# A hybrid encoder layer on one core: residual and its squares by token, gate and up alternating in the FFN's first group

## The chip, the core and the metric

The kernel runs on one core of a Trainium2 chip. The metric is the device time of one execution in microseconds, the median over several executions. The engines are named as in the profile: PE (TensorE, matrix products), DVE (VectorE), ACT (ScalarE), POOL (GpSimd), and SP, which here only issues transfers. Times inside an execution are microseconds from the start of the profiled span.

## What is computed

One transformer-like layer over 16 meta tokens and 256 sequence tokens with 2048 features, in float32. Cut to what matters here:

```python
def rms_norm(x, g):
    y = x * lax.rsqrt(jnp.mean(x * x, axis=-1, keepdims=True) + EPS)
    return y * g

h = rms_norm(x, g_mix_pre)
u = h @ w_in
...
mix = jnp.concatenate([y_a, y_b, y_c, y_d], axis=-1) @ w_out
x = x + rms_norm(mix, g_mix_post)
h = rms_norm(x, g_ffn_pre)
gate = causal_dwconv(h @ ffn_w_gate, ffn_conv_w, ffn_conv_b)
y = (jax.nn.silu(gate) * (h @ ffn_w_up)) @ ffn_w_down
return x + rms_norm(y, g_ffn_post)
```

The four mixers behind `...` are not touched. `FFN_DIM` is 5632. The result is wanted for the 256 sequence tokens alone. The convolution over three tokens needs the two tokens before them, so that from w_out on the kernel carries 258 columns: 2 meta tokens and 256 others.

## The kernel before

**Layout.** Activations lie feature-major: a tile of 128 partitions (features) by 258 columns (tokens) for each of 16 feature blocks k. `mo` holds the mixers' output after w_out, `xT` the layer's input and later the new x, `hh` and `hl` the high and low part of the normalised x times its gain. Two tensors lie token-major, [128 tokens, 2 halves i, 2048 features]: `xtok`, the residual that is added at the very end, and the DRAM input `x_tok`.

**Products.** Each float32 product is made of three passes: high weight by high activation (L202), high by low (L203), low by high (L204). A weight tile is 128 x 2048 (1 MB): 4 feature blocks of input (a chunk c) by 4 output blocks f, 48 matmuls in `tile_matmuls`. SP's queue loads it (`load`, three buffers `raw`), ACT writes its high part (`whi`, L148), DVE its low part (`wlo`, L154), each in two halves, one tile ahead of PE. Where a tile is the last of its sum (c = 3), `tile_matmuls` goes block by block through all four k, otherwise by halves.

**Order.** The stages are w_in, the mixers, w_out (16 tiles), then the norm after the mixers, the FFN in 11 groups j of four tiles of gate and four of up, the 44 tiles of w_down, the last norm and the output. Side work is written as Python generators that `step` advances between tiles. A scheduler may move instructions, but from `strict` to `strict.close()` DVE and ACT keep the written order. PSUM has four banks for `acc` tiles (gate) and four for `mx` tiles (up, transposes, statistics).

**Between w_out and the FFN.** `rstd_columns` sums the squares of `mo` by matmuls with ones (L231), DVE and ACT make the reciprocal root (L239 to L252, L246), `rstd_spread` (L255) spreads it over all partitions into the PSUM tile `mrstd`. `new_x(k)` multiplies `mo` by `mrstd` on DVE (L936) and adds it to `xT` (L937, on DVE for k below 2, otherwise on POOL). `new_h(k)` makes `hh` on ACT (L940) and `hl` on DVE (L941). `turned` transposes four 128 x 128 blocks on PE (L920) into one bank, `keep` copies that to `xtok` on ACT (L924). `keep_warm` (L302) issues products of ones whose result nobody reads.

**The first group, j = 0.** After its four gate tiles `ffn_stats` starts: 16 squares of the new x on ACT (L969, L972), added up by DVE and POOL in turn into `ssum` (L973), then the columns' sums on PE (L231), the root, and the spread (L255) into free columns of the gate banks, copied to `rstd2`. `finish(j)` multiplies the group's gate and up sums by `rstd2` and makes `yT` (L1005 to L1013). Gate and up are linear in h, so the statistics are needed only in `finish`.

**The residual.** `xtok` gets, for the features 1024 to 2047, the transposed `mo` before its norm, which `residual` multiplies by the token's rstd and adds to `x_tok` (L994). For the features 0 to 1023 it gets the transposed new x (L920 and L924 again, in the tiles of group j = 1). `x_tok` holds 1024 features of each token and is loaded by SP's queue over the memory of `mo` (L986) once the last `new_x` has read it.

Of the kernel before, what the change touches and what calls it, by code (L numbers as in the profile page):

```python
# [6 lines left out]
F32 = mybir.dt.float32  # L7
F32R = mybir.dt.float32r
AF = mybir.ActivationFunctionType
ALU = mybir.AluOpType  # L10
AX = mybir.AxisListType

P = 128
# [13 lines left out]
PRE = 4  # L27
OUT_CUTS = ((0, 256), (256, 256), (512, 512), (1024, 512), (1536, 512))
AHEAD = (1, 2, 4)
WARM = (9, 2, 2)  # L30
PIECES = (4, 2, 2, 2)
LATER = 1
BIG = 1e30
NOT_ADMISSIBLE = -3.0e38
TAKEN = -3.39e38
# [39 lines left out]
def bcast(ap, dims):  # L75
    return bass.AP(tensor=ap.tensor, offset=ap.offset, ap=[ap.ap[0], *dims])
# [3 lines left out]
def hybrid_layer(ctx: ExitStack, tc, t):  # L80
# [14 lines left out]
    def acc():  # L95
        return pacc.tile([P, 512], F32, tag="acc", name="acc")

    def mix_ps():
        return pmix.tile([P, 512], F32, tag="mx", name="mx")
# [17 lines left out]
        queue += [t["w_out"][4 * f + m] for m in range(4)]  # L117
    NJ = FT // 4
    for j in range(NJ):
        queue += [t["w_gate"][4 * j + c] for c in range(4)]  # L120
        queue += [t["w_up"][4 * j + c] for c in range(4)]
    queue += [t["w_down"][k] for k in range(FT)]
    halves = {}
    raws = {}
# [100 lines left out]
    def rstd_columns(small, sq, scale, segs, ps, meanwhile=None):  # L225

        n_seg, ng = len(segs), len(sq)
        order = [(g, j, i) for g in range(ng) for j in range(len(sq[g])) for i in (1, 2, 0)]
        for g, j, i in order:
            c0, n = segs[i]  # L230
            mm(ps[0:n, g * n_seg + i:g * n_seg + i + 1], sq[g][j][:, c0:c0 + n], ones[:, 0:1],  # L231
               start=(g, j, i) == order[0], stop=(j == len(sq[g]) - 1), skip_group_check=True)
        w = ng * n_seg
        v = small.tile([P, 4, 8], F32, tag="rs", bufs=2, name="rs")
        G.memset(v, 1.0)
        n0 = segs[0][1]
        pv = ps[:, 0:w].rearrange("p (g s) -> p g s", g=ng)
        vv = v[:, 0, 0:w].rearrange("p (g s) -> p g s", g=ng)
        V.tensor_scalar(vv[0:n0, :, 0:1], pv[0:n0, :, 0:1], scale, EPS, op0=ALU.mult, op1=ALU.add)  # L239
        V.tensor_scalar(vv[:, :, 1:n_seg], pv[:, :, 1:n_seg], scale, EPS, op0=ALU.mult, op1=ALU.add)  # L240
        rsqrt(v[:, 0, 0:w], v[:, 1, 0:w], v[:, 2, 0:w], v[:, 3, 0:w], meanwhile)
        return v[:, 2, 0:w]
# [11 lines left out]
    def rstd_spread(y, i, n, out):  # L254
        nc.tensor.transpose(out, y[0:n, i:i + 1].to_broadcast([n, P]), ident[0:n, 0:n])  # L255
# [42 lines left out]
    def keep_warm(n):  # L298

        ps = mix_ps()  # L300
        for _ in range(n):
            mm(ps[:, 0:P], ones, ones, start=True, stop=True)  # L302

    keep_warm(WARM[0])
    for c in range(3):
        load(c)
    nc.sync.dma_start(xr[3], t["xT"][:, 12:16, :])
# [609 lines left out]
    def turned(src, i, k0, ps):  # L917

        for j in range(4):
            nc.tensor.transpose(ps[:, j * P:(j + 1) * P], src[:, k0 + j, SEGQ[i + 1][0]:SEGQ[i + 1][0] + P], ident)  # L920
        return xtok[:, i, k0 * P:(k0 + 4) * P], ps

    def keep(dst, ps):
        act(dst, ps, AF.Copy)  # L924


    keep_warm(WARM[1])
    for i in range(2):
        keep(*turned(mo, i, 8, mix_ps()))
    for i, (c0, n) in enumerate(SEGQ):  # L930
        rstd_spread(y, i, n, mrstd[:, c0:c0 + n])
    later = [turned(mo, i, 12, mix_ps()) for i in range(2)]
    keep_warm(WARM[2])

    def new_x(k):
        V.tensor_tensor(mo[:, k, :], mo[:, k, :], mrstd[:, :LQ], ALU.mult)  # L936
# [27 lines left out]
    gens.append(["new_h", new_hs(), None])  # L964

    def ffn_stats(gate):
        for k in range(KT):
            if k == 0:
                pin(act(ssum, xT[:, k, :], AF.Square))  # L969
            else:  # L970
                sq = T.tile([P, LQ], F32, tag="tsq", bufs=2, name="tsq")
                pin(act(sq, xT[:, k, :], AF.Square))  # L972
                pin((G if k % 2 else V).tensor_tensor(ssum, ssum, sq, ALU.add))  # L973
            if k % 4 == 3:
                yield

        y = rstd_columns(T, [[ssum]], 1.0 / D, SEGQ, gate[3][:, 264:272])
        yield
        for i, (c0, n) in enumerate(SEGQ):
            rstd_spread(y, i, n, gate[i][:, 264:264 + n])  # L980
            act(rstd2[:, c0:c0 + n], gate[i][:, 264:264 + n], AF.Copy)

    def residual():

        x2 = bcast(mo, [[D // 2, 2], [1, D // 2]])
        nc.sync.dma_start(x2, t["x_tok"])  # L986
        for i in range(2):
            keep(*turned(xT, i, 0, acc()))
            yield
            keep(*turned(xT, i, 4, acc()))  # L990
            yield
        for i in range(2):
            dst = xtok[:, i, D // 2:D]
            V.scalar_tensor_tensor(dst, dst, y[:, i + 1:i + 2], x2[:, i, :], op0=ALU.mult, op1=ALU.add)  # L994
            yield

    feats = lambda k: (hh[:, k, :], hl[:, k, :])
    feats2 = lambda k: (hh[:, k, 2:LQ], hl[:, k, 2:LQ])
# [25 lines left out]
    tmp = F  # L1024
    for j in range(NJ):
        gate = [acc() for _ in range(4)]
        for c in range(4):
            tile_matmuls(gate, feats, list(range(4 * c, 4 * c + 4)), LQ, True, c == 0, c == 3)
        if j == 0:
            drain("new_h")  # L1030
            strict.close()
            gens.append(["ffn_stats", ffn_stats(gate), None])
        up = [mix_ps() for _ in range(4)]
        for c in range(4):
            tile_matmuls(up, feats2, list(range(4 * c, 4 * c + 4)), SEQ, True, c == 0, c == 3)
        if j == 0:
            drain("ffn_stats")
            gens.append(["residual", residual(), None])
        finish(j, gate, up)
        if j == NJ - 3:  # L1040
            drain("residual")
            tst.close()
            Y = ctx.enter_context(tc.tile_pool(name="down_in", bufs=1, side="right"))
            gpost_row = Y.tile([P, D], F32, name="gpost_row")
            G.dma_start(gpost_row, bass.AP(tensor=t["rows"].tensor, offset=t["rows"].offset + 32, ap=[[0, P], [1, D]]))
            ys = {0: ysplit(0), 1: ysplit(1)}
# [60 lines left out]
def layout(inputs):  # L1107
    import numpy as np

    f = {k: np.asarray(v) for k, v in inputs.items()}  # L1110
    a = {}
    h = np.concatenate([f["meta_tokens"], f["x"][0]], axis=0)
    a["xT"] = h.T.reshape(KT, P, L).transpose(1, 0, 2)

    a["x_tok"] = f["x"][0].reshape(2, P, D).transpose(1, 0, 2)[:, :, D // 2:]

    def cols_of(v, n):
        return v.reshape(n, P).T

    cw = f["ssd_conv_w"][0]  # L1120
    fw = f["ffn_conv_w"][0]
    i = np.arange(P)[:, None]
    mask15 = np.where(i % 2 == 0, -BIG, 0.0)
    a["cols"] = np.concatenate([
        cols_of(f["norm_mix_pre"][0], 16), cols_of(f["norm_mix_post"][0], 16), cols_of(f["norm_ffn_pre"][0], 16),
        cw.reshape(4, 8, P).transpose(2, 1, 0).reshape(P, 32), cols_of(f["ssd_conv_b"][0], 8),
        cols_of(f["ssd_norm"][0], 4), cols_of(f["pool_scale"][0], 4), f["dsa_kv_norm"][0][:, None],
        cols_of(np.repeat(f["ssd_d"][0], HD), 4),
        fw.reshape(3, FT, P).transpose(2, 1, 0).reshape(P, 3 * FT), cols_of(f["ffn_conv_b"][0], FT), mask15,
        i % 2 == np.array([0, 1]), i % 16 <= np.array([14, 15]), i // 16 == np.arange(H)], axis=1).astype(np.float32)  # L1130
    a["rows"] = np.concatenate([f["ssd_dt_bias"][0], f["fox_f_bias"][0], f["ssd_a_log"][0], np.zeros(8, np.float32),
                                f["norm_ffn_post"][0]])[None]
    p = i.T
    head = np.where(p % 32 < 4, 8 + p // 32 * 2 + p % 32 // 2, -1)
    a["consts"] = np.concatenate([np.eye(P), i <= p, i == head, i == p // 16, i == p % 16], axis=1).astype(np.float32)

    def tiles(w):
        k, n = w.shape
        return w.reshape(k // 512, 4, P, n // 512, 512).transpose(3, 0, 2, 1, 4).reshape(-1, P, 2048)

    w_in = f["w_in"][0]
    parts = []
    for g in ORDER:
        for c, n in W_IN_GROUPS[g]:
            parts.append(np.zeros((D, n), np.float32) if c is None else w_in[:, c:c + n])
    a["w_in"] = tiles(np.concatenate(parts, axis=1))
    w_out = f["w_out"][0]
    a["w_out"] = tiles(np.concatenate([w_out[P * MIX_ROWS[m]:P * MIX_ROWS[m] + 512] for m in MIX_ORDER], axis=0))
    a["w_gate"] = tiles(f["ffn_w_gate"][0])
    a["w_up"] = tiles(f["ffn_w_up"][0])  # L1150
    a["w_down"] = f["ffn_w_down"][0].reshape(FT, P, D)
    a["w_uk"] = f["dsa_w_uk"][0].transpose(1, 0, 2).reshape(P, 512)
    a["w_uv"] = f["dsa_w_uv"][0].transpose(1, 0, 2).reshape(P, 512)
    a["pool_w"] = f["pool_w"][0].transpose(1, 0, 2)
    return {k: np.ascontiguousarray(v) for k, v in a.items()}
# [15 lines left out]
```

## Time and profile before

| what | value |
|---|---|
| median of three executions | 1162.54 us (1160.34 to 1163.70) |
| the profiled execution | 1161.08 us |
| its span, first to last instruction | 1159.3 us |
| what lies around the span | 1.8 us |
| PE busy, matmuls | 1136.5 us, 98% |
| DVE busy | 721.6 us, 62% |
| ACT busy | 541.6 us, 47% |
| POOL busy | 56.0 us, 5% |
| mean granted clock of PE | 0.993 of full speed |
| moved by the DMA queues | 207.34 MB, 179 GB/s in the mean |

The busy shares are averages over very different stages. A time at which PE waits or runs at a lower granted clock is found in the timeline of PE and in the windows, which give for a stretch the busy time of each engine and the granted clock (1.00 is 2.4 GHz, 0.50 is 1.2 GHz).

### The profile page before, as it was taken

Reading aid. Unit: us, or ns where it says so; the run is one execution under the profiler, and the core shown is the slowest. Engines: PE = TensorE matmul, PEld = TensorE weight load, DVE = VectorE, ACT = ScalarE, POOL = GpSimd, SP = SyncE. Lnnn points to the kernel's source line nnn. Section 1 sums busy time; section 2 is a strip of 40 time slices with the busy share of each in tenths; the row PEclk is TensorE's granted clock in tenths of the full one; section 3 lists DMA queues with packets and bytes.
Section 4 is the critical chain, followed back from the end, with each engine's and each line's share of the span. In section 5 each row is a group of like instructions: output and inputs, shape, how many; then the busy total and the mean of one; then the engine's idle time right before and its main releaser. Section 6 shows DMA issues by size and latency. Waiting matters only on the chain.

```text
span 1159.3 us, 19938 instructions
## 1 busy us (share of the span) xinstructions
PE 1136.5 (98%) x8331; PEld 1068.6 (92%) x8331; DVE 721.6 (62%) x1150; ACT 541.6 (47%) x767; POOL 56.0 (5%) x64
## 2 busy tenths in 40 slices
PE   7999999999999989999999999999999999999997
PEld 7999989998999989999999999999999888888885
DVE  8885675778755876655565566555655655445564
ACT  6434363564544655544444444444444444444452
POOL 6000010000000430000000000000000000000000
PEclk9999999999999999999999999999999999999998
DMA  7644444435655354555555554555555555555542
GB/s 271 215 146 146 166 149 164 146 115 180 219 191 183 144 208 150 214 183 182 182 183 183 184 182 179 190 186 183 182 193 187 190 182 182 184 192 196 190 181 73
DMA packets 32762, 207.34 MB, mean 179 GB/s; under 512 B 3712, under 2 KB 4896, under 8 KB 9376
## 3 DMA queue, kind: packets, MB, share of 16 engines
q1 hardware_dynamic: 30528, 198.80, 48.0%
q0 software_dynamic: 1568, 6.48, 1.8%
q8 instruction: 65, 1.06, 0.4%
q10 hardware_dynamic: 576, 0.79, 0.2%
q14 instruction: 25, 0.20, 0.1%
HBM read 203.93 MB, written 2.12 MB: 178 GB/s over the span
## 4 chain that ended last, share of the span: by engine, by line
PE 63%; DVE 1%; POOL 0%; ACT 0%; issue 0%; DVEq 0%; ACTq 0%; POOLq 0%
PE mx L203 7%; PE mx L202 7%; PE mx L204 7%; PE acc L204 7%; PE acc L203 7%; PE acc L202 7%; PE acc L1060 4%; PE acc L1061 4%; PE acc L1059 4%; PE mx L1061 3%; PE mx L1060 3%; PE mx L1059 3%; POOL ssum L973 0%; DVE yo L1089 0%; DVE yo L1103 0%
## 5 line engine op out<-in xcount | busy, mean ns | idle before, releaser
L154 DVE TENSOR_TENSOR wlo<-raw,whi 128x1024 fp32r<-128x1024 f32 (+2 forms) x373 | 455.7, 1226 | 343.4 <-ACT whi L148 342.1
L148 ACT ACTIVATE whi<-raw 128x1024 fp32r<-128x1024 f32 (+2 forms) x373 | 386.8, 1046 | 476.2 <-PE acc L203 226.2
L203 PE MATMUL acc<-hl,whi 128*128 128x258 f32 x704 | 199.2, 283 | 1.0 <-DVE hl L941 0.9
L203 PE MATMUL mx<-hl,whi 128*128 128x256 f32 x704 | 199.3, 283 | 0.0
L202 PE MATMUL mx<-hh,whi 128*128 128x256 f32 x704 | 199.2, 283 | 0.0
L204 PE MATMUL acc<-hh,wlo 128*128 128x258 f32 x704 | 199.1, 283 | 0.0
L204 PE MATMUL mx<-hh,wlo 128*128 128x256 f32 x704 | 198.7, 282 | 0.0
L202 PE MATMUL acc<-hh,whi 128*128 128x258 f32 x704 | 198.2, 283 | 0.2 <-ACT hh L940 0.2
L202 PE MATMUL acc<-xh,whi 128*128 128x272 f32 (+1 forms) x576 | 171.6, 298 | 1.0 <-ACT whi L148 1.0
L204 PE MATMUL acc<-xh,wlo 128*128 128x272 f32 (+1 forms) x576 | 166.3, 291 | 4.3 <-DVE wlo L154 4.3
L203 PE MATMUL acc<-xl,whi 128*128 128x272 f32 (+1 forms) x576 | 166.9, 290 | 0.5 <-DVE xl L315 0.5
L203 PEld LDWEIGHTS acc<-hl,whi 128*128 128x128 f32 x704 | 133.3, 189 | 1.8 <-DVE hl L941 1.6
L203 PEld LDWEIGHTS mx<-hl,whi 128*128 128x128 f32 x704 | 133.8, 190 | 0.0
L204 PEld LDWEIGHTS mx<-hh,wlo 128*128 128x128 f32 x704 | 133.7, 190 | 0.0
L202 PEld LDWEIGHTS mx<-hh,whi 128*128 128x128 f32 x704 | 133.4, 189 | 0.0
L202 PEld LDWEIGHTS acc<-hh,whi 128*128 128x128 f32 x704 | 132.5, 189 | 0.4 <-ACT hh L940 0.4
L204 PEld LDWEIGHTS acc<-hh,wlo 128*128 128x128 f32 x704 | 132.8, 189 | 0.0
L202 PEld LDWEIGHTS acc<-xh,whi 128*128 128x128 f32 x576 | 110.5, 192 | 7.1 <-issue 4.6
L204 PEld LDWEIGHTS acc<-xh,wlo 128*128 128x128 f32 x576 | 109.7, 192 | 5.5 <-DVE wlo L154 5.0
L203 PEld LDWEIGHTS acc<-xl,whi 128*128 128x128 f32 x576 | 110.4, 192 | 1.7 <-issue 0.9
L1061 PE MATMUL acc<-wlo,yh 128*128 128x512 f32 x176 | 69.6, 396 | 0.0
L1060 PE MATMUL acc<-whi,yl 128*128 128x512 f32 x176 | 69.6, 396 | 0.0
(375 smaller groups left out, 1506.5 us busy)
## 6 DMA issues: line engine op xcount, KB each, us to landing
raw<-w_gate SPq DMA_DIRECT2D x44, 1024.0 KB, 4.8
raw<-w_up SPq DMA_DIRECT2D x44, 1024.0 KB, 4.8
raw<-w_down SPq DMA_DIRECT2D x44, 1024.0 KB, 4.8
raw<-w_in SPq DMA_DIRECT2D x32, 1024.0 KB, 4.8
raw<-w_out SPq DMA_DIRECT2D x16, 1024.0 KB, 4.8
raw<-w_in SPq DMA_DIRECT2D x6, 512.0 KB, 7.8
xT<-xT POOLq DMA_DIRECT2D x1, 2064.0 KB, 12.0
xr<-xT SPq DMA_DIRECT2D x4, 272.0 KB, 7.2
```

The costliest lines, as they stand in the source:

```text
L148: act(hi[:, c], src, AF.Copy)
L154: V.tensor_tensor(lo, src, hi, ALU.subtract)
L202: mm(accs[f][:, :n], hi[:, c], xh, start=st, stop=False)
L203: mm(accs[f][:, :n], hi[:, c], xl, start=False, stop=False)
L204: mm(accs[f][:, :n], lo[:, c], xh, start=False, stop=en)
L1059: mm(o, yh, hi[:, c], start=(k == 0), stop=False)
L1060: mm(o, yl, hi[:, c], start=False, stop=False)
L1061: mm(o, yh, lo[:, c], start=False, stop=(k == FT - 1))
```

## The change

The changed kernel does three things. (1) All 16 blocks of `mo` are transposed between w_out and the FFN (32 transposes, where there were 16), and the 16 transposes of the new x in group j = 1 are gone, and so are the two calls of `keep_warm` between w_out and the FFN. (2) `x_tok` has all 2048 features (2 MB), POOL's queue loads it, and `ffn_stats` makes the residual by token on DVE, squares it on ACT with a sum along the row, and joins to that the sums of the two meta columns, which come from `xT`. (3) The first group takes its tiles in the order gate 0, gate 1, up 0, up 1, gate 2, gate 3, up 2, up 3, and `ffn_stats` starts after the fourth of these. Behind the places named, lines move on by two or three.

```diff
+FFN_ORDER = ([(w, c) for h in (0, 2) for w in ("w_gate", "w_up") for c in (h, h + 1)],
+             [(w, c) for w in ("w_gate", "w_up") for c in range(4)])
...
-        queue += [t["w_gate"][4 * j + c] for c in range(4)]
-        queue += [t["w_up"][4 * j + c] for c in range(4)]
+        queue += [t[w][4 * j + c] for w, c in FFN_ORDER[min(j, 1)]]
...
-    keep_warm(WARM[1])
-    for i in range(2):
-        keep(*turned(mo, i, 8, mix_ps()))
+    for k0 in (0, 4):
+        for i in range(2):
+            keep(*turned(mo, i, k0, mix_ps()))
     for i, (c0, n) in enumerate(SEGQ):
         rstd_spread(y, i, n, mrstd[:, c0:c0 + n])
-    later = [turned(mo, i, 12, mix_ps()) for i in range(2)]
-    keep_warm(WARM[2])
+    keep(*turned(mo, 0, 8, mix_ps()))
+    later = [turned(mo, i, k0, mix_ps()) for i, k0 in ((1, 8), (0, 12), (1, 12))]
...
     def ffn_stats(gate):
-        for k in range(KT):
-            if k == 0:
-                pin(act(ssum, xT[:, k, :], AF.Square))
-            else:
-                sq = T.tile([P, LQ], F32, tag="tsq", bufs=2, name="tsq")
-                pin(act(sq, xT[:, k, :], AF.Square))
-                pin((G if k % 2 else V).tensor_tensor(ssum, ssum, sq, ALU.add))
-            if k % 4 == 3:
-                yield
-
-        y = rstd_columns(T, [[ssum]], 1.0 / D, SEGQ, gate[3][:, 264:272])
+        x2 = bcast(mo, [[D, 2], [1, D]])
+        G.dma_start(x2, t["x_tok"])
+        for _ in range(3):
+            yield
+        sums = HP.tile([P, 3, 2], F32, name="sums")
+        junk = HP.tile([P, D // 2], F32, name="junk")
+        for half in range(2):
+            c = slice(half * D // 2, (half + 1) * D // 2)
+            for i in range(2):
+                dst = xtok[:, i, c]
+                V.scalar_tensor_tensor(dst, dst, y[:, i + 1:i + 2], x2[:, i, c], op0=ALU.mult, op1=ALU.add)
+                act(junk, dst, AF.Square, accum_out=sums[:, half, i:i + 1])
+            yield
+
+        sq = HP.tile([P, KT, 2], F32, name="sq")
+        act(sq, xT[:, :, 0:2], AF.Square)
+        V.tensor_reduce(sums[:, 2, :], sq.rearrange("p k t -> p t k"), axis=AX.X, op=ALU.add)
+        mm(gate[3][0:2, 264:265], sums[:, 2, :], ones[:, 0:1], start=True, stop=True, skip_group_check=True)
+        v = HP.tile([P, 4, 8], F32, name="rs2")
+        G.memset(v, 1.0)
+        V.tensor_tensor(v[:, 1, 1:3], sums[:, 0, :], sums[:, 1, :], ALU.add)
+        V.tensor_scalar(v[:, 0, 1:3], v[:, 1, 1:3], 1.0 / D, EPS, op0=ALU.mult, op1=ALU.add)
+        V.tensor_scalar(v[0:2, 0, 0:1], gate[3][0:2, 264:265], 1.0 / D, EPS, op0=ALU.mult, op1=ALU.add)
+        rsqrt(v[:, 0, 0:3], v[:, 1, 0:3], v[:, 2, 0:3], v[:, 3, 0:3])
         yield
         for i, (c0, n) in enumerate(SEGQ):
-            rstd_spread(y, i, n, gate[i][:, 264:264 + n])
+            rstd_spread(v[:, 2, 0:3], i, n, gate[i][:, 264:264 + n])
             act(rstd2[:, c0:c0 + n], gate[i][:, 264:264 + n], AF.Copy)
-
-    def residual():
...
+        up = None
+        for n, (w, c) in enumerate(FFN_ORDER[min(j, 1)]):
+            if w == "w_gate":
+                tile_matmuls(gate, feats, list(range(4 * c, 4 * c + 4)), LQ, True, c == 0, c == 3)
+            else:
+                up = up or [mix_ps() for _ in range(4)]
+                tile_matmuls(up, feats2, list(range(4 * c, 4 * c + 4)), SEQ, True, c == 0, c == 3)
+            if j == 0 and n == 3:
+                drain("new_h")
+                strict.close()
+                gens.append(["ffn_stats", ffn_stats(gate), None])
...
-    a["x_tok"] = f["x"][0].reshape(2, P, D).transpose(1, 0, 2)[:, :, D // 2:]
+    a["x_tok"] = f["x"][0].reshape(2, P, D).transpose(1, 0, 2)
```

The compiled programs show where the scheduler put things. PE between w_out and the FFN, before (L920 is a transpose, L231 the sums of squares, L255 the spread, L302 a product of ones):

```order
L302 MATMUL mx<-ones 128x128 x2
L920 MATMUL mx<-cst,mo 128x128
L231 MATMUL mx<-ones,slast 128x1 x2
L231 MATMUL mx<-ones,slast 2x1
L920 MATMUL mx<-cst,mo 128x128 x7
L255 MATMUL mx<-cst,rs 128x2
L255 MATMUL mx<-cst,rs 128x128 x2
L920 MATMUL mx<-cst,mo 128x128 x8
L302 MATMUL mx<-ones 128x128 x2
```

The same place now; the lines are L922, L233, L257:

```order
L922 MATMUL mx<-cst,mo 128x128 x5
L233 MATMUL mx<-ones,slast 128x1 x2
L233 MATMUL mx<-ones,slast 2x1
L922 MATMUL mx<-cst,mo 128x128 x11
L257 MATMUL mx<-cst,rs 128x2
L257 MATMUL mx<-cst,rs 128x128 x2
L922 MATMUL mx<-cst,mo 128x128 x16
```

Sixteen transposes now stand ahead of the spread and sixteen behind it, where eight and eight stood.

PE in the third FFN tile, which is now up 0, with numbers (`mx_4564` to `mx_4567` are up's four banks, `whi_4492` and `wlo_4493` the first half of the tile):

```order
2762 L204 MATMUL mx_4566<-hh_4339,whi_4492 128x256
2763 L205 MATMUL mx_4566<-hl_4340,whi_4492 128x256
2764 L206 MATMUL mx_4566<-hh_4339,wlo_4493 128x256
2765 L204 MATMUL mx_4567<-hh_4339,whi_4492 128x256
2766 L205 MATMUL mx_4567<-hl_4340,whi_4492 128x256
2767 L206 MATMUL mx_4567<-hh_4339,wlo_4493 128x256
```

The tile begins with number 2747, and number 2765, its nineteenth matmul, is the first that writes up's fourth bank; that bank is the one in which `mrstd` lies, which DVE reads in all sixteen of `new_x`. In the kernel before, up's first matmul stood two tiles later.

DVE around the residual, before, behind the last `hl` (L994 is the residual, two instructions for half of the features; numbers run on from the program's start):

```order
486 L154 TENSOR_TENSOR wlo_4615<-raw_4546,whi_4614 128x1024
487 L154 TENSOR_TENSOR wlo_4643<-raw_4546,whi_4642 128x1024
488 L994 SCALAR_TENSOR_TENSOR xtok_4333<-xtok_4333,rs_4317,mo_3190 128x1024 x2
489 L154 TENSOR_TENSOR wlo_4678<-raw_4612,whi_4677 128x1024
490 L973 TENSOR_TENSOR ssum_3191<-ssum_3191,tsq_4709 128x258
491 L154 TENSOR_TENSOR wlo_4716<-raw_4612,whi_4715 128x1024
```

And now (L980 is the residual, four instructions for all features):

```order
486 L156 TENSOR_TENSOR wlo_4637<-raw_4568,whi_4636 128x1024
487 L156 TENSOR_TENSOR wlo_4665<-raw_4568,whi_4664 128x1024
488 L986 TENSOR_REDUCE sums_4810<-sq_4878 128x2
489 L156 TENSOR_TENSOR wlo_4696<-raw_4634,whi_4695 128x1024
490 L980 SCALAR_TENSOR_TENSOR xtok_4333<-xtok_4333,rs_4317,mo_3190 128x1024 x2
491 L156 TENSOR_TENSOR wlo_4725<-raw_4634,whi_4724 128x1024
492 L980 SCALAR_TENSOR_TENSOR xtok_4333<-xtok_4333,rs_4317,mo_3190 128x1024 x2
493 L156 TENSOR_TENSOR wlo_4755<-raw_4693,whi_4754 128x1024
```

Number 491, the low half of the sixth FFN tile's second half, stands behind the first pair that reads `x_tok`. In this part of the program POOL's order is now the last additions of `new_x`, then the issue of the load of `x_tok`; the eight additions of L973 on POOL are gone.

## Rows read from the trace of the kernel before

**Rows 1.** the page, busy time of the engines

```profile
PE 1136.5 (98%) x8331; PEld 1068.6 (92%) x8331; DVE 721.6 (62%) x1150; ACT 541.6 (47%) x767; POOL 56.0 (5%) x64
```

**Rows 2.** PE's waits: waiter, releaser, total us, times, longest us

```profile
PE mx L573 <- DVE s L570: 2.0, 1, 2.0
...
PE acc L203 <- DVE hl L941: 0.9, 1, 0.9
```

**Rows 3.** windows: stretch, us, busy us (instructions), granted clock, DMA share, GB/s

```profile
400.86:414.30 13.44, 12.41 (x98) 11.91 (x97) 13.36 (x18) 5.67 (x8) 3.39 (x4) 1.00 0.58 201
...
414.30:442.44 28.14, 25.81 (x203) 25.33 (x202) 17.16 (x32) 17.01 (x34) 9.65 (x8) 0.94 0.48 172
...
174.00:176.00 2.00, 2.00 (x10) 2.00 (x10) 0.86 (x2) 1.28 (x3) 0.30 (x1) 0.50 0.65 184
...
434.00:436.00 2.00, 2.00 (x11) 2.00 (x10) 0.00 (x0) 0.00 (x0) 0.00 (x0) 0.50 0.29 119
```

**Rows 4.** timeline of PE, w_out to FFN: start, us, instruction, count, [idle before]

```profile
383.86 0.71 PE L302 MATMUL mx<-ones 128*128 128x128 f32 x4
...
386.70 0.55 PE L255 MATMUL mx<-cst,rs 2*128 2x2 f32 x3 [0.65 <-DVE rs L252]
...
387.09 1.04 PE L920 MATMUL mx<-cst,mo 128*128 128x128 f32 x8
...
388.77 0.74 PE L202 MATMUL acc<-hh,whi 128*128 128x258 f32 x4 [0.20 <-ACT hh L940]
```

**Rows 5.** timeline of ACT, the same stretch

```profile
385.67 1.07 ACT L924 ACTIVATE xtok<-mx 128x512 f32<-128x512 f32 x2
...
388.21 0.51 ACT L940 ACTIVATE hh<-xT,cols 128x258 fp32r<-128x258 f32 x1 [1.47 <-DVE xT L937]
```

**Rows 6.** timeline of DVE, the first FFN group

```profile
404.19 0.41 DVE L936 TENSOR_TENSOR mo<-mo,mx 128x258 f32<-128x258 f32 x1
...
405.06 1.76 DVE L154 TENSOR_TENSOR wlo<-raw,whi 128x1024 fp32r<-128x1024 f32 x1
...
411.75 2.47 DVE L994 SCALAR_TENSOR_TENSOR xtok<-xtok,rs,mo 128x1024 f32<-128x1024 f32 x2
...
414.74 1.23 DVE L154 TENSOR_TENSOR wlo<-raw,whi 128x1024 fp32r<-128x1024 f32 x1 [0.53 <-ACT whi L148]
...
433.74 0.16 DVE L252 SCALAR_TENSOR_TENSOR rs<-rs 128x3 f32<-128x3 f32 x1
...
441.94 0.43 DVE L1005 TENSOR_TENSOR gs<-acc,rstd 128x258 f32<-128x258 f32 x1
```

**Rows 7.** timeline of PE, the end of the first group's statistics

```profile
431.11 0.73 PE L231 MATMUL acc<-ones,ssum 128*128 128x1 f32 x6 [2.33 <-POOL ssum L973]
...
436.33 0.58 PE L255 MATMUL acc<-cst,rs 2*128 2x2 f32 x3
```

**Rows 8.** timeline of PE, the fourth gate tile of group j = 1

```profile
459.72 0.28 PE L202 MATMUL acc<-hh,whi 128*128 128x258 f32 x1
...
462.51 0.66 PE L920 MATMUL acc<-cst,xT 128*128 128x128 f32 x4
...
467.63 0.28 PE L202 MATMUL mx<-hh,whi 128*128 128x256 f32 x1
```

**Rows 9.** timeline of POOL, its last two additions of new_x

```profile
403.94 1.80 POOL L937 TENSOR_TENSOR xT<-xT,mo 128x258 f32<-128x258 f32 x2 [1.50 <-DVE mo L936]
```

**Rows 10.** DMA issues: what, queue, count, KB each, us to landing

```profile
mo<-x_tok SPq DMA_DIRECT2D x1, 1024.0 KB, 5.3
...
gpost_row<-rows POOLq DMA_DIRECT2D x1, 1024.0 KB, 5.9
...
xT<-xT POOLq DMA_DIRECT2D x1, 2064.0 KB, 12.0
...
e<-drow POOLq DMA_DIRECT2D x1, 1024.0 KB, 7.0
```

More of the change, by code (lines that the diff above doesn't have):

```diff
@@ L29 @@
 AHEAD = (1, 2, 4)
-WARM = (9, 2, 2)
+WARM = 9
 PIECES = (4, 2, 2, 2)
 LATER = 1
+FFN_ORDER = ([(w, c) for h in (0, 2) for w in ("w_gate", "w_up") for c in (h, h + 1)],
+             [(w, c) for w in ("w_gate", "w_up") for c in range(4)])
 BIG = 1e30
@@ L302, in keep_warm @@
             mm(ps[:, 0:P], ones, ones, start=True, stop=True)
-    keep_warm(WARM[0])
+    keep_warm(WARM)
     for c in range(3):
@@ L978, in ffn_stats @@
+        V.tensor_scalar(v[0:2, 0, 0:1], gate[3][0:2, 264:265], 1.0 / D, EPS, op0=ALU.mult, op1=ALU.add)
+        rsqrt(v[:, 0, 0:3], v[:, 1, 0:3], v[:, 2, 0:3], v[:, 3, 0:3])
         yield
         for i, (c0, n) in enumerate(SEGQ):
-            rstd_spread(y, i, n, gate[i][:, 264:264 + n])
+            rstd_spread(v[:, 2, 0:3], i, n, gate[i][:, 264:264 + n])
             act(rstd2[:, c0:c0 + n], gate[i][:, 264:264 + n], AF.Copy)
-    def residual():
[L985 to L995, printed above, removed]
@@ L1026, in hybrid_layer @@
         gate = [acc() for _ in range(4)]
[L1027 to L1035, printed above, removed]
+        up = None
[9 more added lines that the diff above has]
+                gens.append(["ffn_stats", ffn_stats(gate), None])
         if j == 0:
             drain("ffn_stats")
-            gens.append(["residual", residual(), None])
         finish(j, gate, up)
         if j == NJ - 3:
-            drain("residual")
             tst.close()
```

## The prediction

> **What bounds the kernel now.** I read the page first: PE is busy for 98% of the span and DVE for 62% [rows 1]. So work moved between DVE, ACT and POOL is worth nothing by itself. Time is won where PE waits, runs at a lower clock, or does work that can go. The view of PE's waits lists few after w_out: 0.9 us for `hl` in the gate tiles, and a longer one that the timeline of PE shows as 2.33 us before L231, for `ssum` of POOL [rows 2, 7]. The windows, cut at the first matmul of FFN tiles, give the stages [rows 3]. Fifth to eighth tile (up of group 0) take 28.14 us. The pace to hold against that is the first three gate tiles of group 1: from 442.44, where the window ends, to 459.72 [rows 3, 8], 17.28 / 3 = 5.76 us a tile, 0.120 a matmul of 258 columns. A tile of up, with 256 columns, is then 5.76 x 256/258 = 5.72 us. Four are 22.9, so this stage loses 5.2: the wait, six small L231, a spread, and a fall of the clock: 432 to 436 us holds a stretch at a granted clock of 0.50 (1.2 GHz) [rows 3]. The third and fourth gate tile lose 13.44 - 2 x 5.76 = 1.9 us [rows 3]. The fourth gate tile of group 1 lasts 467.63 - 459.72 = 7.91 us, 2.1 above pace, for the 16 transposes within it [rows 8].
>
> **Transition (w_out to FFN).** Sixteen more transposes come in, four products of ones go (two times some 0.7 us; one shown) [rows 4]. A transpose costs 1.04/8 = 0.13 us [rows 4]. Ahead of the spread, eight more take about 1.0 us against 0.7 for the products that go, and 0.65 us of PE's idle time stood there [rows 4]: the spread stays at 386.7. Behind it 16 take 2.1 us where 8 and the products lasted until 388.57, the start of the 0.20 idle before 388.77 [rows 4]. By PE alone they would end at 389.2; four wait at a time for an ACT copy (1.07 the pair [rows 5]) that frees their bank. The next to gate on `hl` is DVE, which has lost nothing; the first `hh` moves by one ACT copy at most, 0.53, with 1.47 idle ahead of it [rows 5]. Bounds 0 and 0.6; I take a loss of 0.1, since the second matmul group waited for `hl` anyway.
>
> **Third and fourth tile.** With up 0 and up 1 in their place, PE needs `hl` of k = 0 to 7 only, and the waits for the later ones, 1.9 us, go. Something else takes their place: up's fourth bank is `mrstd`'s, which DVE reads last at 404.19 + 0.41 = 404.60 [rows 6]. The nineteenth matmul of the third tile wants it: 400.86 [rows 3] + 18 x 0.119 = 403.0. That is a new wait of 1.6 us. Behind it two tiles of up are 11.44 + 1.6 = 13.04 instead of 13.44: gain 0.4, less the 0.1 above; bounds 0 to 1.9. The wait lies between one of 0.92 (`hl`) behind which no lower clock shows and one of 1.97 behind which 174 to 176 ran at 0.50 [rows 2, 3]. I take no fall, and keep the fall as a rival.
>
> **Statistics.** Three small L231, a pass over ACT and fifteen additions go. In their place PE has one small matmul: 0.73/6 [rows 7], with its filling 0.2. The spread keeps its 0.4. The four tiles, two of gate and two of up, last 2 x 5.76 + 2 x 5.72 + 0.6 = 23.6 instead of 28.14 [rows 3]: **gain 4.5**. For that DVE must be done when the spread comes, by the compiled order 24 matmuls into the eighth tile. In before DVE came from L231 (431.11) to L252's end, 433.90, in 2.8 us with one `wlo` between [rows 6, 7]; now the matmul stands right before those 24, whose 2.9 us cover that. If this cover fails, PE waits some tenths.
>
> **x_tok.** The load leaves POOL after its last addition, 403.94 + 1.80 = 405.74 [rows 9]. Before, SP's queue brought 1 MB in 5.3 us; POOL's queue brought 1 MB in 5.9 and 7.0, and 2 MB of `xT` in 12.0 [rows 10]. Doubled and added: it lands between 405.74 + 10.6 = 416.3 and 405.74 + 14.0 = 419.7, by `xT` at 417.7. The DVE order puts `wlo` of the sixth tile's second half behind the first pair of residuals: 2.47 + 1.23 = 3.7 us after the landing [rows 6]. PE wants it in the ninth matmul of the sixth tile (a last tile of gate goes through all k of a block): 400.86 + 13.04 + 0.1 + 5.76 + 8 x 0.12 = 420.7. So PE waits from a landing at 417.0 on. Bounds 0 and 2.7; I take 0.3, between what the SP row and the `xT` row give. Other `wlo` behind the second pair come 1 us or more before they are needed. The four squares on ACT have as many columns as the sixteen before and lie beside PE.
>
> Here the Trainium skill speaks, in "DMA: Bandwidth & Descriptors", "Anatomy of one DMA — SWDGE (gpsimd) path": some 2 us fixed and then 436 GB/s, by which 2 MB would land in an estimated 6.8 us and the 0.3 would be 0. The row of `xT`, 12.0 us, disagrees.
>
> **Group 1.** Its 16 transposes go: 7.91 - 5.76, **gain 2.1** [rows 8]. The eight copies on ACT have moved to the transition, where they are counted.
>
> **Finish of group 0.** It shares DVE and ACT with the splits, as before. `gs` of the fourth block ended at 442.37 [rows 6], 0.07 us before tile 9 began. Now everything is some 5 us earlier, PE included, so this is as tight as before: PE wants the fourth gate bank 32 matmuls into its tile, 3.8 us later. Bounds 0 and 1.6; I take 0.
>
> **Sum.** -0.1 + 0.4 + 4.5 - 0.3 + 2.1 = 6.6 us. Against the profiled execution, 1161.08, that is 1154.5; against the median of the runs, 1162.54, it is 1155.9. I take the middle of these two, 1161.8, as the kernel's time, and so forecast **1155.2 us**. What can be told from no change is 0.3%, 3.5 us: faster is below 1158.3, slower above 1165.3.
>
> **Rivals.**
>
> *Clock falls at the new wait.* If 1.6 us of idle time on PE is enough, a stretch of matmuls behind it goes at 1.2 GHz. The stage with the 2.33 us wait prices that: 5.2 lost, less the wait itself, 0.7 of L231 and 0.4 of the spread, leaves 1.8. Then 1157.0. For it: 1.6 is nearer to 1.97 than to 0.92. Against: the wait falls into a stretch with PE otherwise full. Chance 0.22.
>
> *Finish is late.* The third and fourth `gs` come behind a `wlo` and the load of the Silu table, and PE waits up to 1.6 in group 1's first tile: 1156.8. Against: PE reaches that bank late. Chance 0.08.
>
> *x_tok comes at the slowest rate.* By the 7.0 row it lands at 419.7, PE waits 2.7 instead of 0.3 and the clock falls for 1.8: gain 6.6 - 4.2 = 2.4, time 1159.4, within 0.3%. For it: three weight tiles of 1 MB are on the way at the same time. Chance 0.14.
>
> *x_tok comes so late that the kernel is slower.* DVE is busy without a gap until 411.8, its first residual row [rows 6]. If POOL gets to send its transfer only then, the load lands at 411.8 + 12.0 = 423.8, and with half a weight tile's time in front (2.4) at 426.2. PE then waits 9.2 instead of 0.3 and the clock falls for 1.8: 6.6 - 10.7 = 4.1 lost, 1165.9. It decides from the landing: behind 422.1 (a wait of 5.1) nothing is gained, behind 425.6 the kernel is slower by over 0.3%. For it: `wlo` took 1.76 us while POOL added and 1.23 when it did not [rows 6], so the two hinder each other. Against: POOL's additions hold POOL, a transfer's issue needs it briefly; `gpost_row` landed in 5.9 beside a DVE that was splitting weights. Chance 0.06.
>
> The Trainium skill has this in "SBUF — State Buffer", "SBUF: two separate sides": transfers issued from GpSimd have their descriptors written by GpSimd, which DVE's two-port instructions lock out, whereas SP's are safe. The two lengths of `wlo` agree with such a shared port; the 5.9 of `gpost_row` shows no lock.
>
> That the change does not do what it says can't be excluded for the alternation alone: it swaps one wait for another, which is in the sum, at 0.4.
>
> **Chances.** Forecast 0.50, the four rivals 0.22, 0.08, 0.14, 0.06. Faster by over 0.3%: 0.50 + 0.22 + 0.08 = 0.80. Within: 0.14. Slower: 0.06. The range goes down by the 0.3 of x_tok, by 0.6 of the third tile's wait and by the runs' spread of about 1.5 around their median: 1152.8. Up it holds the first three rivals and a bit of spread: 1160.0.
>
> **What would show it.** Right: first gate matmul within 0.3 of 388.8; a wait of 1.6 before an `mx` matmul at about 404.6, clock 1.00 behind it; no wait for `ssum`, fifth to eighth tile 23.6 to 24; no transposes (L922) behind the first gate matmul; group 1's gate tiles 5.76 each. Wrong: a landing of `x_tok` behind 418 with a wait for `wlo` in the sixth tile; a clock of 0.50 between 404 and 412; a wait for `gs` in group 1's first tile; a first gate matmul behind 389.4.

## The result and the profile after

Over seven executions the median went from 1162.93 to 1155.11 us. The ratio is 0.9941 with a 95% interval of 0.9921 to 0.9960: faster by 4.7 to 9.2 us. One of the seven executions of the changed kernel took 1476.17 us at a granted clock of 0.694 and is left out of the ratio. The forecast was 1155.2 in a range of 1152.8 to 1160.0.

The profiled execution has a span of 1154.3 us, 5.0 below before. What lies ahead of the change differs by chance, in code that is the same: the first sum of the norm after w_out (L231, now L233) starts at 384.77 instead of 383.31. Of before, PE's timeline:

```profile
383.31 0.62 PE L231 MATMUL mx<-ones,ssum 128*128 128x1 f32 x6
```

So all that follows is measured from that first sum, on PE's timeline, to the first `up` matmul of group 1: the **stretch**. It holds everything that the change touches. In before it is 467.63 [rows 8] - 383.31 = 84.32 us, now 462.51 - 384.77 = 77.74: 6.58 us less. What lies behind it is the same, 1159.3 - 467.63 = 691.7 and 1154.3 - 462.51 = 691.8.

The windows of the changed kernel: FFN tiles 3 and 4, 5 to 8, and the gate tiles of group 1, then two windows around the new wait (columns as in [rows 3], which has the first two stages of before):

```profile
402.29:415.47 13.18, 11.73 (x98) 11.52 (x97) 12.27 (x18) 6.19 (x9) 3.95 (x5) 1.00 0.72 275
...
415.47:439.25 23.78, 23.78 (x199) 23.46 (x198) 16.52 (x25) 14.18 (x22) 0.56 (x1) 1.00 0.80 291
...
439.25:462.51 23.26, 23.26 (x194) 23.20 (x193) 18.73 (x34) 14.91 (x23) 0.00 (x0) 1.00 0.48 167
...
404.00:406.00 2.00, 0.61 (x6) 0.40 (x4) 2.00 (x5) 1.35 (x2) 0.65 (x1) 1.00 0.24 29
...
406.00:408.00 2.00, 1.94 (x16) 1.94 (x17) 2.00 (x3) 1.32 (x4) 1.70 (x3) 1.00 0.76 270
```

13.18 stands against 13.44, 23.78 against 28.14, 23.26 against the 25.19 between 442.44 [rows 3] and 467.63 [rows 8]. Around the new wait PE was busy for 0.61 of 2 us, and the granted clock stayed at 1.00.

PE's timeline of the changed kernel at the places of [rows 4] and [rows 7], with the new wait between:

```profile
384.77 0.62 PE L233 MATMUL mx<-ones,ssum 128*128 128x1 f32 x6
...
388.11 0.55 PE L257 MATMUL mx<-cst,rs 2*128 2x2 f32 x3 [0.21 <-DVE rs L254]
...
388.50 1.95 PE L922 MATMUL mx<-cst,mo 128*128 128x128 f32 x16
...
390.20 0.74 PE L204 MATMUL acc<-hh,whi 128*128 128x258 f32 x4
...
404.33 0.28 PE L206 MATMUL mx<-hh,wlo 128*128 128x256 f32 x1
...
406.06 0.39 PE L204 MATMUL mx<-hh,whi 128*128 128x256 f32 x1 [1.45 <-DVE mo L938]
...
432.82 0.19 PE L987 MATMUL acc<-ones,sums 128*2 128x1 f32 x2
...
435.97 0.58 PE L257 MATMUL acc<-cst,rs 2*128 2x2 f32 x3
...
462.51 0.28 PE L204 MATMUL mx<-hh,whi 128*128 128x256 f32 x1
```

From the first sum to the first gate matmul: 390.20 - 384.77 = 5.43 us, before 388.77 [rows 4] - 383.31 = 5.46, with 16 transposes more. The wait for `ssum` is gone, the spread at 435.97 has no wait, and a wait of 1.45 us for DVE's last reading of `mrstd` is new.

DVE, POOL and the load of `x_tok` in the changed kernel, to compare with [rows 6, 9, 10]:

```profile
405.59 0.41 DVE L938 TENSOR_TENSOR mo<-mo,mx 128x258 f32<-128x258 f32 x1
...
416.31 2.48 DVE L980 SCALAR_TENSOR_TENSOR xtok<-xtok,rs,mo 128x1024 f32<-128x1024 f32 x2 [1.30 <-DMA mo<-x_tok]
...
407.45 0.58 POOL L971 DMA_DIRECT2D mo<-x_tok  x1 [0.30 <-POOL xT L939]
...
mo<-x_tok POOLq DMA_DIRECT2D x1, 2048.0 KB, 8.8
```

The load lands 8.8 us behind its issue; DVE stands idle for it for 1.30 us, PE does not.

### The profile page after: what moved, and what is told of

Read it like the earlier page. It is cut to its first block, busy times and chain, and to the rows that moved or that the text cites. A ratio compares the mean times of both kernels' runs of the same rounds, so it can differ in the third digit from the quotient of the medians.

```text
span 1154.3 us, 19891 instructions
## 1 busy us (share of the span) xinstructions
PE 1132.6 (98%) x8319; PEld 1065.5 (92%) x8319; DVE 721.3 (62%) x1147; ACT 540.7 (47%) x760; POOL 47.4 (4%) x57
## 4 chain that ended last, share of the span: by engine, by line
PE 77%; DVE 3%; ACT 1%; issue 1%; DVEq 0%; ACTq 0%
PE acc L204 11%; PE acc L206 11%; PE acc L205 11%; PE mx L204 7%; PE mx L205 7%; PE mx L206 7%; PE acc L1062 4%; PE acc L1063 4%; PE acc L1061 4%; PE mx L1062 3%; PE mx L1063 3%; PE mx L1061 3%; DVE wlo L156 1%; DVE mo L938 0%; DVE hl L943 0%
## 5 line engine op out<-in xcount | busy, mean ns | idle before, releaser
L1061 PE MATMUL acc<-whi,yh 128*128 128x512 f32 x176 | 69.6, 396 | 0.0
```

What stands on the lines that cost most here:

```text
L1061: mm(o, yh, hi[:, c], start=(k == 0), stop=False)
```

## The experiments

All runs are compared over the stretch and three of its stages, read off PE's timeline in one profile each. The transition from the first sum to the first gate matmul (5.43 to 5.47 us) and the first two FFN tiles (12.08 to 12.09) are the same everywhere and are left out.

| kernel | tiles 3, 4 | tiles 5 to 8 | gate, group 1 | stretch | ratio of time to before (95%) |
|---|---|---|---|---|---|
| before | 13.44 | 28.14 | 25.19 | 84.32 | |
| changed | 13.18 | 23.78 | 23.26 | 77.74 | 0.9941 (0.9921 to 0.9960) |
| changed, again (e8) | 13.17 | 23.78 | 23.26 | 77.73 | 0.9946 (0.9929 to 0.9962) |
| without the alternation (e1) | 13.44 | 23.69 | 23.27 | 77.92 | 0.9935 (0.9915 to 0.9955) |
| alternation alone (e5) | 13.20 | 25.13 | 25.19 | 81.08 | 0.9973 (0.9960 to 0.9986) |
| transposes alone (e7) | 13.45 | 32.59 | 23.08 | 86.63 | 1.0018 (1.0002 to 1.0033) |
| alternation and transposes (e11) | 13.18 | 26.96 | 23.09 | 80.74 | 0.9986 (0.9969 to 1.0003) |
| fourth block last (e3; e9) | 11.91; 11.89 | 23.78; 23.78 | 23.25; 23.24 | 76.46; 76.43 | 0.9936 (0.9917 to 0.9955); 0.9947 (0.9928 to 0.9966) |
| banks turned, no effect (e4) | 13.22 | 23.78 | 23.25 | 77.76 | 0.9948 (0.9928 to 0.9969) |
| x_tok on SP (e2) | 13.21 | 23.79 | 23.27 | 77.79 | 0.9962 (0.9947 to 0.9977) |
| x_tok late (e6) | 13.19 | 29.96 | 23.27 | 83.93 | 1.0012 (0.9997 to 1.0027) |
| bank wanted earlier (e10) | 15.75 | 23.78 | 23.25 | 80.30 | 0.9971 (0.9961 to 0.9980) |

**Without the alternation (e1).** `FFN_ORDER[0]` is that of the other groups:

```diff
-FFN_ORDER = ([(w, c) for h in (0, 2) for w in ("w_gate", "w_up") for c in (h, h + 1)],
+FFN_ORDER = ([(w, c) for w in ("w_gate", "w_up") for c in range(4)],
```

> Everything of the change but the alternation: group 0 takes gate 0 to 3, then up 0 to 3. Theory (the alternation only swaps one wait for another): third and fourth FFN tile 13.4 us, with the waits for hl back and no wait for mrstd's bank, against 13.2 with the change; fifth to eighth tile 23.8, fourth gate tile of group 1 5.8; time 1155.4, within 1 us of the changed kernel. Rival (the alternation makes the room in which the statistics are hidden): fifth to eighth tile 25 us or more with a wait of PE for wlo, the spread or rstd2; time 1157 or more.

PE's timeline of this kernel has the old wait back, and no wait for the bank:

```profile
406.20 0.39 PE L205 MATMUL acc<-hl,whi 128*128 128x258 f32 x1 [0.92 <-DVE hl L943]
```

The stretch is 0.18 us longer than with the change. In the changed kernel the alternation swaps one wait for another and is worth next to nothing, as the theory said.

**The alternation alone (e5).** Before, with the new `FFN_ORDER` and the loop over it, and nothing else.

> The kernel before with the alternation alone. Theory: the 0.9 us wait for hl becomes one of 1.5 us for mrstd's bank in the third tile, third and fourth tile 13.2 us; the wait for ssum (2.3 us) and the low clock behind it stay, fifth to eighth tile 28; transposes in group 1 stay, 25.2 for its gate tiles; time 0.3 us below the kernel before, not to be told from it. Rival (the alternation carries the gain): fifth to eighth tile 24 to 25, time 1158.

The theory failed here: the stretch is 3.24 us shorter than before, not 0.3. PE's timeline shows the bank's wait as expected, but no wait for `ssum` any more, and 0.60 us for the spread in its place:

```profile
403.14 0.39 PE L204 MATMUL mx<-hh,whi 128*128 128x256 f32 x1 [1.48 <-DVE mo L938]
...
427.20 0.73 PE L233 MATMUL acc<-ones,ssum 128*128 128x1 f32 x6
...
431.56 0.58 PE L257 MATMUL acc<-cst,rs 2*128 2x2 f32 x3 [0.60 <-DVE rs L254]
```

ACT's timeline says why. In before, the split and the first square on ACT, and the last addition on POOL:

```profile
413.65 1.06 ACT L148 ACTIVATE whi<-raw 128x1024 fp32r<-128x1024 f32 x1 [5.31 <-PE acc L203]
...
414.62 0.40 ACT L969 ACTIVATE ssum<-xT 128x258 f32<-128x258 f32 x1
...
429.60 1.46 POOL L973 TENSOR_TENSOR ssum<-ssum,tsq 128x258 f32<-128x258 f32 x1 [0.90 <-ACT tsq L972]
```

and in this kernel:

```profile
409.77 1.06 ACT L150 ACTIVATE whi<-raw 128x1024 fp32r<-128x1024 f32 x1 [1.80 <-PE mx L205]
...
410.74 0.40 ACT L971 ACTIVATE ssum<-xT 128x258 f32<-128x258 f32 x1
...
426.38 0.76 POOL L975 TENSOR_TENSOR ssum<-ssum,tsq 128x258 f32<-128x258 f32 x1 [0.61 <-DVE ssum L975]
```

In before, the split ahead of the first square waits 5.31 us for PE to give a `whi` buffer back: the fourth tile, the last of gate, goes block by block through all four k, so both halves are needed to the tile's end. In the alternated order the fourth tile is an up tile that is not the last of its sum and goes by halves, and the wait is 1.80. Measured from the first sum, the first square starts at 410.74 - 381.79 = 28.95 instead of 414.62 - 383.31 = 31.31, 2.4 us earlier. From there to the end of the last addition the chain is as long as before, 427.14 - 410.74 = 16.40 us against 431.06 - 414.62 = 16.44, so `ssum` is ready 2.4 us earlier. That is the 2.33 us that PE waited for it, and without that wait the clock stays up (1.00 in every window from 424 to 440 us).

**The transposes alone (e7).** The transition of the change and the residual by token for all features (four L994, 2 MB of `x_tok` on POOL's queue), with the old squares, additions and order.

> The transposes and the residual by token for all features (2 MB of x_tok on POOL's queue), but the old squares, additions and order. Theory: transition unchanged at 5.4 us from the first sum to the first gate matmul, group 1's gate tiles 23.0 instead of 25.2, the wait for ssum stays at 2.3 to 5 us (two more residual instructions of 1.2 us each stand in DVE's order among the additions), fifth to eighth tile 28 to 31; time 1161 to 1163.5, a gain of 2.1 at most. Rival (the 16 transposes moved to the transition cost PE there what they save in group 1): transition 7.5 us, time 1163 to 1165.

The transition takes 5.43 us with the 16 transposes more, and the gate tiles of group 1 are 2.11 us shorter, as the theory had it. The wait for `ssum` grows beyond what was expected. Of this kernel, PE, and ahead of it the first square, the residual and the last addition:

```profile
434.67 1.14 PE L231 MATMUL acc<-ones,ssum 128*128 128x1 f32 x6 [6.04 <-POOL ssum L973]
...
414.46 0.40 ACT L969 ACTIVATE ssum<-xT 128x258 f32<-128x258 f32 x1
...
414.84 2.97 DVE L993 SCALAR_TENSOR_TENSOR xtok<-xtok,rs,mo 128x1024 f32<-128x1024 f32 x2 [3.18 <-DMA mo<-x_tok]
...
433.15 1.46 POOL L973 TENSOR_TENSOR ssum<-ssum,tsq 128x258 f32<-128x258 f32 x1 [0.91 <-ACT tsq L972]
```

The residual stands in DVE's order ahead of the additions, waits 3.18 us for `x_tok`, and the additions wait with it; two more residuals stand among them further on. The chain from the first square to the last addition takes 434.61 - 414.46 = 20.15 us, 3.71 more than before, and by the same 3.71 PE's wait grows, from 2.33 to 6.04. Tiles 5 to 8 take 4.45 us more than before. By itself this part makes the kernel slower.

**Alternation and transposes, old statistics (e11).** The two edits above together.

> The alternation and the transposes, with the old squares and additions: all of the change but the sums by token. If the parts simply add up from the two runs that had one part each, the first sum to the first up tile of group 1 takes 84.3 - 3.2 + 2.3 = 83.4 us. Theory (the old chain of additions is long, and x_tok's later landing stands in DVE's order among them, but the alternation starts it 2.4 us earlier): wait of PE for ssum 1 to 4 us, stretch 79 to 83. Rival (with alternation the old statistics are hidden as well, and the sums by token bring nothing): stretch 78 us or less, no wait for ssum.

PE, the first square, the first pair of residuals, the last addition, and two windows behind PE's wait:

```profile
432.50 0.72 PE L233 MATMUL acc<-ones,ssum 128*128 128x1 f32 x6 [1.89 <-POOL ssum L975]
...
414.23 0.41 ACT L971 ACTIVATE ssum<-xT 128x258 f32<-128x258 f32 x1
...
416.83 2.99 DVE L995 SCALAR_TENSOR_TENSOR xtok<-xtok,rs,mo 128x1024 f32<-128x1024 f32 x2 [0.18 <-DMA mo<-x_tok]
...
431.71 0.74 POOL L975 TENSOR_TENSOR ssum<-ssum,tsq 128x258 f32<-128x258 f32 x1 [0.61 <-DVE ssum L975]
...
432.00:434.00 2.00, 1.50 (x13) 1.45 (x14) 1.46 (x2) 2.00 (x3) 0.45 (x1) 1.00 0.66 279
...
434.00:436.00 2.00, 2.00 (x20) 2.00 (x18) 2.00 (x4) 0.61 (x2) 0.00 (x0) 1.00 0.13 29
```

The stretch, 80.74 us, is shorter than the two parts added up give (83.4). The earlier start alone does not explain that, since it is in the alternation's 3.2 already. The rows show two things more: the chain from the first square to the last addition is 432.45 - 414.23 = 18.22 us long instead of 20.15, with the residual waiting 0.18 us for `x_tok` instead of 3.18, and the wait of 1.89 us has no lower clock behind it. The sums by token bring 80.74 - 77.74 = 3.0 us on top of it, and 86.63 - 77.92 = 8.7 where the alternation is missing.

**The fourth block last (e3, e9).** In the first tile of up, the twelve matmuls of the fourth block come behind the 36 of the other three:

```diff
+            elif wait_f3:
+                for kk in range(2):
+                    for f in range(3):
+                        pair(f, part, kk)
+                if part == 1:
+                    for k in range(4):
+                        pair(3, k // 2, k % 2)
             else:
```

> The changed kernel, with the twelve matmuls of the fourth block of up 0 behind the 36 of the other three blocks in that tile. Theory (the 1.5 us wait there is for mrstd's bank alone, and nothing else is late behind it): no wait for the bank, third and fourth tile 11.5 to 11.7 us instead of 13.2, the rest as with the change; time 1153.6, ratio to before 0.992. Rival (something else is late next: hl for gate 2, wlo, or x_tok): third and fourth tile as said, but a new wait of about 1.5 us in the fifth or sixth tile, time 1155.

> The kernel with the twelve matmuls of the fourth block last in up 0, beside the changed kernel on the same chip. Theory: the stretch from the first sum to the first up tile of group 1 is 76.2 us against 77.6, and the median 1.4 us lower; the intervals of the two will overlap, since each is wide by 4 us. Rival (the 1.5 us are given back later in the span): medians the same and the part behind that stretch longer by about 1.4.

The wait for the bank is gone in both profiles, and 0.18 us for `wlo` stand in the tile (here of e3):

```profile
404.59 0.39 PE L206 MATMUL mx<-hh,wlo 128*128 128x256 f32 x1 [0.18 <-DVE wlo L156]
```

The stretch is 1.3 us shorter than that of the changed kernel, and what lies behind it is as long (691.7 to 691.8 us in e3, e8 and e9). So nothing is late behind it and nothing is given back. The medians (1153.42 beside 1153.13 for the changed kernel on the same chip) do not resolve 1.3 us. By the traces this is the shortest version.

> The changed kernel itself, beside the next one on the same chip. From the first sum of the norm after w_out to the first up tile of group 1: 77.6 us as in its first profile; time 1154 to 1156.

Its stretch repeats to 0.01 us. Its median, 1153.13, is below what was expected; the kernel before took 1159.92 on the same chip, and 1162.93 where the change was first measured.

**A longer wait for the bank (e4, e10).** The first try turned the list of up's banks:

```diff
-                up = up or [mix_ps() for _ in range(4)]
+                if not up:
+                    up = [mix_ps() for _ in range(4)]
+                    up = up[3:] + up[:3] if j == 0 else up
```

> The changed kernel with up's four banks turned by one, so that mrstd's bank is wanted by the first matmul of the third tile and not by its nineteenth. Theory (an idle time of PE of 1.5 us costs only itself here, one of 2 us and more also a stretch at 1.2 GHz): wait 3.4 to 3.7 us, granted clock near 0.5 in some 2 to 4 us behind it, third and fourth tile 13.2 + 2.1 + 1.8 = 17.1 us; time 3.9 above the changed kernel, 1159. Rival (the clock does not fall for a single wait of this length): 15.3 us, time 1157.

In the trace the wait stands at the same place in the tile all the same, 402.78 - 399.00 = 3.78 us behind its start (3.77 in the changed kernel), and is 1.48 us long: the edit did not do what was meant. So this run tells nothing on the clock, and is one more repeat of the changed kernel. The second try pinned the matmuls of that tile in the order of the blocks (`late` off for it):

> The changed kernel with the first half of up 0 in the order of its blocks, kept by a pin, so that mrstd's bank is wanted by the tenth matmul and not by the nineteenth. Theory (the wait lasts until DVE's last reading of mrstd wherever PE meets it; of this length it costs the clock too): wait 2.5 us; clock of 0.5 for about 3.5 us behind it; third and fourth tile 13.2 + 1.8 = 15.0 us (nine matmuls come behind the wait instead of ahead of it, which adds 1.1 by itself, the low clock 1.8: 16.1 at most); time 2 to 3 above the changed kernel. Rival (the clock stays): 14.3 us, time 1.1 above it.

PE's timeline and two windows of it:

```profile
407.05 0.38 PE L205 MATMUL mx<-hh,whi 128*128 128x256 f32 x1 [2.53 <-DVE mo L939]
...
408.00:410.00 2.00, 2.00 (x14) 2.00 (x13) 2.00 (x4) 1.42 (x3) 0.72 (x2) 0.65 1.17 434
...
410.00:412.00 2.00, 2.00 (x12) 2.00 (x11) 2.00 (x5) 0.28 (x1) 0.00 (x0) 0.50 0.86 320
```

The wait is 2.53 us, and the clock falls behind it. Tiles 3 and 4 take 2.57 us more: nine matmuls that now stand behind the wait, 1.08, and 1.5 for the low clock. This is the rival of the fallen clock, at a wait one microsecond longer than the one of the change.

**x_tok on SP's queue (e2).** `nc.sync.dma_start` in place of `G.dma_start`.

> The changed kernel with x_tok on SP's queue, between the weight tiles, instead of POOL's. Theory (the queue does not matter as long as the landing is in time): issue near 407 behind the last new_x, landing 5.5 to 10 us later, no wait of PE for wlo in the fifth or sixth tile, first sum to the first up tile of group 1 77.6 us as with the change; time within 1.5 us of the changed kernel. Rival A (DVE holds up what GpSimd has to write for its own transfers): landing 3 us or more earlier than with POOL's queue, 6 us after the issue. Rival B (SP stands still until mo is free and the weights behind it come late): a wait of PE for wlo or whi of 1 us or more in the seventh tile, time 1156 or more.

The load takes 8.2 us instead of 8.8:

```profile
mo<-x_tok SPq DMA_DIRECT2D x1, 2048.0 KB, 8.2
```

The stretch is 77.79, as with the change. The queue does not matter in this stretch. (The interval of its time reaches above that of the changed kernel, which was not timed on the same chip; the stretch and what lies behind it, 691.7 us, show no loss, and the first sum came at 385.10 in this profile.)

**x_tok late (e6).** Six additions on POOL ahead of the issue:

```diff
+        for _ in range(6):
+            pin(G.tensor_tensor(mo[:, KT - 1, :], mo[:, KT - 1, :], xT[:, KT - 1, :], ALU.add))
         G.dma_start(x2, t["x_tok"])
```

> The changed kernel with six more additions of 258 columns on POOL between its last new_x and the issue of x_tok's load (their result is overwritten by the load). Theory (PE waits for wlo of the sixth tile once x_tok lands later than 33.7 us behind the first sum of the norm after w_out; with the change it lands at 31.5): landing at 36 to 37, a wait of PE for wlo of 2.3 to 3.2 us in the sixth tile, with the clock falling behind it for 1.8 more; fifth to eighth tile 26 to 29 instead of 23.8, time 1157.5 to 1160. Rival (DVE or ACT have more room than the order shows): fifth to eighth tile 24 to 25.

POOL, the load, DVE and PE of this kernel, and two windows of it:

```profile
404.79 6.86 POOL L974 TENSOR_TENSOR mo<-mo,xT 128x258 f32<-128x258 f32 x6
...
mo<-x_tok POOLq DMA_DIRECT2D x1, 2048.0 KB, 9.9
...
421.87 1.28 DVE L982 SCALAR_TENSOR_TENSOR xtok<-xtok,rs,mo 128x1024 f32<-128x1024 f32 x1 [6.78 <-DMA mo<-x_tok]
...
424.35 0.54 PE L206 MATMUL acc<-hh,wlo 128*128 128x258 f32 x1 [4.42 <-DVE wlo L156]
...
424.00:426.00 2.00, 1.65 (x8) 1.66 (x9) 2.00 (x3) 1.70 (x4) 0.00 (x0) 0.61 0.40 82
...
426.00:428.00 2.00, 2.00 (x11) 2.00 (x11) 2.00 (x3) 1.77 (x4) 0.00 (x0) 0.54 0.89 365
```

The additions took 1.14 us each beside a busy DVE, longer than I had priced them, and the load 9.9. So it landed at 421.87 - 382.34 = 39.5 us behind the first sum, later than planned, and PE waited 4.42 us, in the sixth tile and for `wlo`, as the theory said. In this program one residual instead of two stands ahead of that `wlo`, 1.28 + 1.22 = 2.5 us instead of 3.7, so that a landing at 33.7 + 1.2 = 34.9 would have cost nothing, and 4.6 us late gave 4.42. Tiles 5 to 8 grew by 6.18, that is the wait and 1.76 for the low clock behind it.

## Why the prediction was right, point by point

The sum was 6.6 us, the stretch is 6.58 shorter. Agreement to 0.02 is luck: four parts of the sum were off by 0.13 to 0.17 each, two one way and two the other. So is a median within 0.1 of the forecast, as the same kernel took 1153.13 when it was timed again (e8). Term by term:

**Transition.** A loss of 0.1 was taken, 0.03 was gained. The 16 transposes more lie beside DVE's and ACT's work: they end about where the first gate matmul starts, which the profile shows without a wait.

**Third and fourth tile.** A gain of 0.4 was taken, 0.26 came. The wait for the bank was put at 1.6 and is 1.45.

**Statistics.** 4.5 less the 0.3 for `x_tok` was taken, 4.36 came. The size of the term was right, but what it stood for was told incompletely. The text counted the alternation at 0.4 and the whole rest of the stage as the new statistics' doing. The runs show that either of the two removes most of the loss: the alternation alone shortens tiles 5 to 8 by 3.0, the sums by token without alternation (with the transposes, which they need) by 28.14 - 23.69 = 4.45. The sentence that the alternation "swaps one wait for another" holds only where the statistics are short; with the old ones it also starts the squares 2.4 us earlier. I had not looked at what held the first square on ACT.

**x_tok.** 0.3 was taken for a landing near 417, none came. The step that was mis-sized is the load: 8.8 us, where rows of other loads gave 10.6 to 14.0. The 8.5 to 9.9 of all profiles with POOL's queue also stand above the estimate of 6.8 worked out from the Trainium skill ("DMA: Bandwidth & Descriptors", "Anatomy of one DMA — SWDGE (gpsimd) path"), with weight tiles on the way at the same time. What the prediction said of the point from which PE waits was borne out by e6, with the 1.2 us more room that its order of DVE gives.

**Group 1 and `finish`.** 2.1 was taken, 1.93 came. The transposes' time is saved whole: the fourth gate tile takes 5.80 us instead of 7.91. But the first takes 445.15 - 439.25 = 5.90 instead of 448.16 - 442.44 = 5.72. Of before, then of the changed kernel with the third `gs` on DVE:

```profile
448.16 0.28 PE L202 MATMUL acc<-hh,whi 128*128 128x258 f32 x1
```

```profile
445.15 0.28 PE L204 MATMUL acc<-hh,whi 128*128 128x258 f32 x1
...
439.58 0.42 DVE L1007 TENSOR_TENSOR gs<-acc,rstd 128x258 f32<-128x258 f32 x1
```

The runs with the old statistics have 5.72 to 5.73 there (e5, e7, e11), those with the sums by token 5.88 to 5.92. So 0.18 are lost with the sums by token, most likely in `finish`, which was put at nothing because it is "as tight as before": the third `gs` ends at 440.00, and the tile's seventh matmul, which wants its bank, is due at 439.25 + 6 x 0.12 = 439.97. The profile lists no wait there, so this cause is not shown.

**The rivals.** The clock stayed at 1.00 behind the new wait in every profile that has one of 1.45 to 1.48 us; e10 shows that the mechanism was real and its price (1.5 us) near the 1.8 put down. `finish` cost no more than the 0.18 above, where the rival had up to 1.6. The rival on the slower side, a load held up on POOL's queue, did not come: issue at 407.45 and landing 8.8 us later, beside a DVE that was busy for most of that time, and SP's queue needed 8.2 in the same place. The lock that the Trainium skill describes ("SBUF — State Buffer", "SBUF: two separate sides") shows in these loads as no more than what POOL's queue takes above SP's 8.2: 0.3 to 1.7 us over ten profiles (8.5 to 9.9). e6 shows the price of a load 8 us later: 6.2 us, and a kernel no faster than before.

## What to carry to other kernels

Two edits that shorten the same wait don't add up: the alternation is worth 3.2 us alone and 0.2 beside the new statistics, and the transposes lose 2.3 alone and win 0.3 beside the alternation, so a part has to be priced beside the others. Ask not only how long a late chain is, but what held its first instruction: here a buffer that PE gave back late because of the order of matmuls in the tile before. And a change of a few microseconds is read from its own stretch of the trace, which repeats to 0.03 us here, where the medians of the same kernel were 1155.11 and 1153.13.

## What was not expected

The length of a wait of PE alone does not tell whether the clock falls. In the mixers, in code that is the same in all kernels, PE waits for DVE between 0.84 and 2.61 us (L573, later L575, L576 or L582). Two of these waits and the windows behind them, of the kernel with the transposes alone:

```profile
171.77 0.27 PE L573 MATMUL mx<-cst,s 128*16 128x128 f32 x1 [1.61 <-DVE s L570]
...
174.00:176.00 2.00, 2.00 (x10) 2.00 (x10) 0.97 (x2) 1.16 (x3) 0.29 (x1) 0.50 0.68 229
```

and of e9:

```profile
173.76 0.27 PE L582 MATMUL mx<-cst,s 128*16 128x128 f32 x1 [2.04 <-DVE s L579]
...
176.00:178.00 2.00, 2.00 (x19) 2.00 (x18) 0.97 (x2) 1.16 (x3) 0.29 (x1) 1.00 0.71 217
```

1.61 us cost the clock in one, 2.04 us did not in the other; 1.72 (e6) and 1.87 (e5) did not either, 1.97 (before; 2.0 in [rows 2]) did. In the FFN the 1.89 of e11 did not. What tells these apart was not found out. Together with the length of that wait it is part of why the first sum after w_out starts anywhere between 380.34 and 385.76 us in the profiles shown here; the change has no part in that.
